# Weight tiles split into a high and a low part by two GpSimd transfers instead of a staged load, a ScalarE cast and a VectorE subtraction

## The chip, the cores and the metric

The kernel runs on one core of one Trainium2 chip. Its engines are PE (TensorE: matmuls, with PEld for the load of the stationary operand), DVE (VectorE), ACT (ScalarE), POOL (GpSimd) and SP (SyncE, which only issues transfers). Transfers between HBM and the on-chip memory run on 16 DMA engines, from queues of SP, ACT and POOL. Each engine works through its own instructions in order and waits on semaphores for the others. The metric is the device time of one launch in microseconds; lower is better.

## What is computed

A decoder trunk of two layers on one sequence: 512 tokens, width 1024, all in float32. The first layer mixes tokens by a gated DeltaNet, the second by sliding-window attention on a shared K/V; each layer ends with a gated MLP with a short causal convolution.

```python
for layer in range(DEPTH):
    if layer < N_A_LAYERS:
        h = h + gated_deltanet(rmsnorm(h, a_norm_w[i]), a_w_in[i], ..., a_w_out[i])
    else:
        if j == 0:
            k_sh, v_sh = shared_kv(h, kv_norm_w, w_kv)
        h = h + sliding_window_sink_attention(rmsnorm(h, b_norm_w[j]), k_sh, v_sh, b_w_q[j], ..., b_w_o[j], ...)
    h = h + conv_gated_mlp(rmsnorm(h, ffn_norm_w[layer]), ffn_w_up[layer], ..., ffn_w_down[layer])
return rmsnorm(h, final_norm_w)
```

The weight matrices concern us here: `a_w_in` (1024 x 6176), `a_w_out` (2048 x 1024), `w_kv` (1024 x 512), `b_w_q` and `b_w_o` (1024 x 1024 each), and for each layer `ffn_w_up` (1024 x 5632) and `ffn_w_down` (2816 x 1024). Each weight is used once, against all 512 tokens.

## The kernel before

**Precision by three matmuls.** TensorE takes its operands in a rounded form of float32, here type F32R. To keep more of the precision, each operand is split in two: the high part is the value rounded, the low part is the value minus the high part. A product is then three matmuls, high x high, high x low and low x high (`mm3`, lines 132 to 137), all added into one bank of PSUM. Activations are split by `split` and `split_scaled`, weights by `cast`.

**The path of a weight before.** `load_stage` (L116) has SP load a part of a matrix, kt x 128 rows by 256 columns, into a buffer "stage" (two buffers). `cast` (L124) is called twice for each stage, for its left and its right 128 columns: ScalarE writes the rounded high part into a "whi" tile (L128), VectorE the rest into a "wlo" tile (L129), with three buffers each. `mm3` uses a pair of them for kt x 3 matmuls of 128x128 by 128x512. One such pair and its matmuls is called a block below. kt is 8 nearly everywhere; the down projections of the MLPs are cut into pieces of 6 and 5.

**The stages.** The first, to about 480 us, is the DeltaNet mixer: 48 blocks of `a_w_in` (`project`, L234) among many small matmuls, transposes and a triangular solve, in an order that the list `ORDER` gives. Then come the output projection (L776, 16 blocks), the first MLP (`ffn`, L829: 44 up blocks and 32 down blocks), the attention (L954: 4 blocks for K/V, 8 for the queries in between the attention's own work, 8 for the output), the second MLP and the final norm. In the MLP each up block is followed by `up` (L838): VectorE empties the bank (L842), ScalarE and VectorE do the convolution (L845, L847), and ScalarE the activation (L862) or the product's split (L864, L140).

**What sets the order.** A scheduler places the instructions of each engine from the program's order and from priorities, under the number of buffers that each tag has. A tile whose tag has n buffers can be written again once the tile n places before it was used for the last time. Each engine, and so each queue from which an engine issues transfers, then runs in the order that was fixed. POOL before has 47 small instructions, fills and masks, among them fills of the DeltaNet's tiles (L495, L496, L572) and of the attention's key tiles (L960, L961).

The gates' small weights (`gst`, L250) take the same path with 48 columns and their own load.

Of the kernel before, what the change touches and what calls it, by code (L numbers as in the profile page):

```python
# [8 lines left out]
F32 = mybir.dt.float32  # L9
F32R = mybir.dt.float32r  # L10
BF16 = mybir.dt.bfloat16
AF = mybir.ActivationFunctionType
ALU = mybir.AluOpType
# [4 lines left out]
P = 128  # L18
# [6 lines left out]
HQK = 8  # L25
# [16 lines left out]
def kernel(  # L42
# [27 lines left out]
    V, S, G, PE, SP = nc.vector, nc.scalar, nc.gpsimd, nc.tensor, nc.sync  # L70
# [6 lines left out]
    def nm(s):  # L77
        cnt[0] += 1
        return f"{s}_{cnt[0]}"

    wpool = ctx.enter_context(tc.tile_pool(name="weights", bufs=1, side="right"))
# [32 lines left out]


    def load_stage(w, r0, kt, c0):  # L116
        st = wpool.tile([P, 8, 256], F32, tag="stage", bufs=2, name=nm("stage"))
        SP.dma_start(
            st[:, :kt, :],
            w[r0 : r0 + kt * P, c0 : c0 + 256].rearrange("(k p) c -> p k c", p=P),  # L120
        )
        return st

    def cast(st, kt, half, m=P):  # L124
        hi = wpool.tile([P, 8, P], F32R, tag="whi", bufs=3, name=nm("whi"))
        lo = wpool.tile([P, 8, P], F32R, tag="wlo", bufs=3, name=nm("wlo"))
        src = st[:, :kt, half * P : half * P + m]
        S.copy(hi[:, :kt, :m], src)  # L128
        V.tensor_tensor(lo[:, :kt, :m], src, hi[:, :kt, :m].bitcast(F32), op=ALU.subtract)  # L129
        return hi, lo  # L130
# [20 lines left out]
        SP.dma_start(xt[:], x[0, c * P : (c + 1) * P, :])  # L151
        xs.append(xt)
    win = a_w_in[0]
    first = wpool.tile([P, 8, 256], F32, tag="stage", bufs=2, name=nm("stage"))
    for i in range(2):
        cs = slice(HQK * P + i * P, HQK * P + (i + 1) * P)
        SP.dma_start(first[:, :, i * P : (i + 1) * P], win[:, cs].rearrange("(k p) c -> p k c", p=P))
    held_stage = {HQK * P: first}


    ident = const([P, P], s="ident")
# [71 lines left out]
    st = [{} for _ in range(4)]  # L233
    def project(c0, i):  # L234
        if c0 not in held_stage:
            held_stage[c0] = load_stage(win, 0, 8, c0)
        ps = bank("d")
        mm3(ps[:], cast(held_stage[c0], 8, i), KD, xh, xl)
        return ps
# [7 lines left out]


    QKV = 2 * HQK * P + HV * P
    gst = wpool.tile([P, 8, 256], F32, tag="stage", bufs=2, name=nm("gst"))  # L250
    G.memset(gst[:, :, 0:48], 0.0)
    c_b = QKV + HV * P
    S.dma_start(gst[:, :, 0:16], win[:, c_b : c_b + 16].rearrange("(k p) c -> p k c", p=P))
    S.dma_start(gst[:, :, 32:48], win[:, c_b + 16 : c_b + 32].rearrange("(k p) c -> p k c", p=P))
    gw = cast(gst, KD, 0, m=48)
    gps = bank("d")
    mm3(gps[:48, :], gw, KD, xh, xl, m=48)
# [19 lines left out]
    for c in range(NC):  # L277
        cs = slice(c * P, (c + 1) * P)
        V.tensor_tensor_scan(R[32:48, cs], ones[32:48, 0:P], sp_r[32:48, cs], 0.0, op0=ALU.mult, op1=ALU.add)
    for c in range(NC):  # L280
        cs = slice(c * P, (c + 1) * P)
# [494 lines left out]
    for m2 in range(KD // 2):  # L776
        sts = [load_stage(a_w_out[0], 1024 * u, 8, 256 * m2) for u in range(2)]
        for j in range(2):
            m = 2 * m2 + j
            ps = bank("d")  # L780
            for u in range(2):
                w = cast(sts[u], 8, j)
                mm3(ps[:], w, 8, yh[8 * u : 8 * u + 8], yl[8 * u : 8 * u + 8], first=u == 0, last=u == 1)
            V.tensor_tensor(hT[m], hT[m], ps[:], op=ALU.add)
# [44 lines left out]
    def ffn(l, h, last=False):  # L829
# [22 lines left out]
        for t0, t1 in ((0, 12), (12, 22)):  # L852
            gh, gl = [], []
            for t in range(t0, t1, 2):
                if l == 0 and t == 6:
                    bias_rows()
                sg = load_stage(wup, 0, 8, t * P)
                sv = load_stage(wup, 0, 8, DFF + t * P)
                gp, lp = wide("G"), wide("L")
                for j in range(2):  # L860
                    a = up(cast(sg, 8, j), t + j, "ga")
                    S.activation(a[:], a[:], AF.Silu)  # L862
                    b = up(cast(sv, 8, j), NF + t + j, "va")
                    V.tensor_tensor(b[:], a[:], b[:], op=ALU.mult)  # L864
                    split(b[:], gp[:, j, :], lp[:, j, :])
                    gh.append(gp[:, j, :])
                    gl.append(lp[:, j, :])
            ku = (t1 - t0) // 2
            for m2 in range(KD // 2):
                sts = [load_stage(wdn, (t0 + u * ku) * P, ku, 256 * m2) for u in range(2)]  # L870
                for j in range(2):
                    m = 2 * m2 + j
                    ws = [cast(sts[u], ku, j) for u in range(2)]
                    if last and t1 == NF and m == KD - 1:
                        final(h, lambda ps, ts, u: down(ps, ws, ku, gh, gl, ts, u))
                        continue
                    ps = bank("d")
                    for u in range(2):
                        down(ps[:], ws, ku, gh, gl, slice(0, T), u)
                    V.tensor_tensor(h[m], h[m], ps[:], op=ALU.add)  # L880
# [247 lines left out]
```

## Time and profile before

| | |
|---|---|
| time, median of 3 runs | 1462.74 us (1460.52 to 1462.97) |
| the profiled execution | 1458.21 us, span 1456.4 us from the first to the last instruction |
| mean granted TensorE clock | 0.996 |
| instructions | 19,545 |
| HBM read, written | 134.65 MB, 16.80 MB |
| SP's queue of transfers | 160,722 packets, 151.27 MB, 33.3% of the 16 DMA engines' span |

Busy time is the time in which an engine had an instruction in work. Matmuls are pipelined: a single matmul of 128x512 shows some 400 ns while the next one starts earlier, so the rate is read from the distance of starts or of finished blocks, not from the mean of one. "Idle before, releaser" is the time for which an engine stood before an instruction, and what ended the wait. An instruction's line with "q" behind the engine (SPq) is one of the queue that issues. "To landing" is the time from the issue of a transfer to the point at which its data can be used. In the table of windows each row gives a stretch of time, and how long each engine was busy in it.

### The profile page before, as it was taken

To read this page: it belongs to the slowest core of one execution; us is meant where nothing else is said; L and a number is where in the kernel's file an instruction comes from. 1 tells how busy PE (TensorE), PEld (TensorE's weight loads), DVE (VectorE), ACT (ScalarE), POOL (GpSimd) and SP (SyncE) were. 2 spreads that over 40 slices of the span, in tenths; PEclk is the share of its full clock that TensorE was granted. 3 is DMA by queue.
4 is the path that set the end of the run, shared out by engine and by line. 5 is a ranking of instruction groups with operands and counts; after the bars stand their busy time and mean duration, and the time that the engine had idled before them with its cause. 6 is when DMAs were issued, how large, how long until landed. Compare 5 with 4: busy or idle time off the path is not lost.

```text
span 1456.4 us, 19545 instructions
## 1 busy us (share of the span) xinstructions
PE 1432.3 (98%) x7519; PEld 1163.6 (80%) x7519; DVE 953.5 (65%) x1661; ACT 718.9 (49%) x1406; POOL 20.1 (1%) x47
## 2 busy tenths in 40 slices
PE   7999999999999999999999999999999999999998
PEld 5778877888877788888888888877788888888887
DVE  5896885978844436776247765777757774366754
ACT  7764564656646424443224444578744443234433
POOL 1000000000000000000010000000000000000000
PEclk9999999999999999999999999999999999999999
DMA  5334254163366523232232234221132322322222
GB/s 154 92 99 112 78 171 119 59 189 110 98 189 209 163 87 108 69 114 87 87 116 91 83 95 130 89 79 44 58 105 69 116 83 86 122 87 87 94 73 94
DMA packets 163074, 152.71 MB, mean 105 GB/s; under 512 B 24165, under 2 KB 150694, under 8 KB 162982
## 3 DMA queue, kind: packets, MB, share of 16 engines
q1 hardware_dynamic: 160722, 151.27, 33.3%
q8 instruction: 59, 0.97, 0.3%
q10 hardware_dynamic: 2259, 0.20, 0.2%
q14 instruction: 34, 0.27, 0.1%
HBM read 134.65 MB, written 16.80 MB: 104 GB/s over the span
## 4 chain that ended last, share of the span: by engine, by line
PE 95%; DMA 3%; ACT 1%; DVE 1%; issue 0%; ACTq 0%; DVEq 0%; SPq 0%
PE d L135 27%; PE d L137 27%; PE d L136 26%; PE s L585 2%; PE p L1043 1%; PE s L600 1%; PE g L1038 1%; PE s L625 1%; PE p L608 1%; PE s L562 1%; PE p L555 1%; PE s L1013 1%; PE g L450 1%; PE g L671 1%; PE g L375 1%; DMA ol<-od 0%
## 5 line engine op out<-in xcount | busy, mean ns | idle before, releaser
L135 PE MATMUL d<-xh,whi 128*128 128x512 f32 x1192 | 475.8, 400 | 0.1
L137 PE MATMUL d<-xh,wlo 128*128 128x512 f32 x1192 | 473.3, 398 | 0.0
L136 PE MATMUL d<-xl,whi 128*128 128x512 f32 x1192 | 471.6, 396 | 0.0
L128 ACT CAST whi<-stage 128x1024 fp32r<-128x1024 f32 (+2 forms) x236 | 230.5, 979 | 337.6 <-PE d L136 318.6
L129 DVE TENSOR_TENSOR wlo<-stage,whi 128x1024 fp32r<-128x1024 f32 (+2 forms) x236 | 267.3, 1133 | 120.4 <-ACT whi L128 114.3
L137 PEld LDWEIGHTS d<-xh,wlo 128*128 128x128 f32 x1192 | 224.4, 188 | 50.5 <-issue 1.4
L136 PEld LDWEIGHTS d<-xl,whi 128*128 128x128 f32 x1192 | 224.3, 188 | 48.2 <-issue 1.2
L135 PEld LDWEIGHTS d<-xh,whi 128*128 128x128 f32 x1192 | 224.7, 188 | 46.1 <-issue 0.7
L842 DVE TENSOR_TENSOR sz<-d,p6s 128x512 f32<-128x512 f32 x58 | 40.0, 689 | 62.9 <-PE d L137 61.0
L227 DVE SCALAR_TENSOR_TENSOR acc<-d,cwc,acc 128x511 f32<-128x511 f32 (+2 forms) x96 | 70.7, 740 | 9.3 <-ACT acc L224 8.8
L862 ACT ACTIVATE dt<-dt 128x512 f32<-128x512 f32 x44 | 27.8, 632 | 83.5 <-DVE dt L847 83.5
L135 PE MATMUL d<-sy,whi 128*128 128x512 f32 (+1 forms) x148 | 57.6, 390 | 0.0
L137 PE MATMUL d<-sy,wlo 128*128 128x512 f32 (+1 forms) x148 | 57.5, 389 | 0.0
L135 PE MATMUL d<-kT,whi 128*128 128x512 f32 (+1 forms) x146 | 57.5, 396 | 0.0
L136 PE MATMUL d<-sy,whi 128*128 128x512 f32 (+1 forms) x148 | 57.0, 385 | 0.0
L137 PE MATMUL d<-kT,wlo 128*128 128x512 f32 (+1 forms) x146 | 57.0, 390 | 0.0
L136 PE MATMUL d<-qT,whi 128*128 128x512 f32 (+1 forms) x146 | 56.8, 389 | 0.0
L847 DVE SCALAR_TENSOR_TENSOR va<-sz,fcw,va 128x511 f32<-128x511 f32 (+1 forms) x58 | 43.4, 748 | 2.7 <-ACT va L845 1.7
L847 DVE SCALAR_TENSOR_TENSOR dt<-sz,fcw,dt 128x511 f32<-128x511 f32 (+1 forms) x58 | 43.4, 748 | 1.2 <-ACT dt L845 0.2
L842 DVE TENSOR_TENSOR zl<-d,p6s 128x512 f32<-128x512 f32 x30 | 20.7, 689 | 33.4 <-PE d L137 33.1
L507 DVE TENSOR_TENSOR sT<-sT,p6s 64x31 f32<-64x31 f32 (+15 forms) x124 | 40.9, 330 | 2.0
L501 DVE TENSOR_TENSOR p6s<-sN,sT 64x31 f32<-64x31 f32 (+15 forms) x124 | 40.9, 330 | 1.8
(377 smaller groups left out, 2116.8 us busy)
## 6 DMA issues: line engine op xcount, KB each, us to landing
stage<-in_ffn_w_up_dram SPq DMA_DIRECT2D x44, 1024.0 KB, 5.1
stage<-in_a_w_in_dram SPq DMA_DIRECT2D x23, 1024.0 KB, 5.4
stage<-in_ffn_w_down_dram SPq DMA_DIRECT2D x16, 768.0 KB, 4.3
stage<-in_ffn_w_down_dram SPq DMA_DIRECT2D x16, 640.0 KB, 4.1
stage<-in_a_w_out_dram SPq DMA_DIRECT2D x8, 1024.0 KB, 5.0
zd<-sz SPq DMA_DIRECT2D x16, 256.0 KB, 2.1
od<-o SPq DMA_DIRECT2D x16, 256.0 KB, 2.5
stage<-in_b_w_q_dram SPq DMA_DIRECT2D x4, 1024.0 KB, 5.0
```

The costliest lines, as they stand in the source:

```text
L128: S.copy(hi[:, :kt, :m], src)
L129: V.tensor_tensor(lo[:, :kt, :m], src, hi[:, :kt, :m].bitcast(F32), op=ALU.subtract)
L135: PE.matmul(ps, hi[:, k, :m], xh[k], start=first and k == 0, stop=False)
L136: PE.matmul(ps, hi[:, k, :m], xl[k][:], start=False, stop=False)
L137: PE.matmul(ps, lo[:, k, :m], xh[k], start=False, stop=last and k == kt - 1)
L227: V.scalar_tensor_tensor(acc[:, d:], ps[:, : T - d], col, acc[:, d:], op0=ALU.mult, op1=ALU.add)
L501: V.tensor_tensor(tv, N[:, s, s + 1 : 32].unsqueeze(2).to_broadcast([64, n, m]), Tm[:, s : s + 1, 0:m].to_broadcast([64, n, m]), op=ALU.mult,)
L507: V.tensor_tensor(Tm[:, s + 1 : 32, 0:m], Tm[:, s + 1 : 32, 0:m], tv, op=ALU.subtract)
L585: PE.matmul(x[:, si], t[:, i, cs], S0[:, si], start=True, stop=True)
L842: V.tensor_tensor(u[:], ps[:], rs[:], op=ALU.mult)
L847: V.scalar_tensor_tensor(acc[:, d:], u[:, : T - d], tap(2 - d, t), acc[:, d:], op0=ALU.mult, op1=ALU.add)
L862: S.activation(a[:], a[:], AF.Silu)
```

## The change

`load_stage` no longer loads: it hands on the address of the weights in HBM. For the 236 blocks of 128 columns, `cast` now issues a transfer from POOL's queue that reads the weights from HBM and writes them rounded into the high tile (the type differs on the two sides); ScalarE writes the negative of the high tile into the low tile; and a second transfer from POOL's queue reads the same weights from HBM again and adds them to the low tile. VectorE has no part in it. The high and the low tiles have four buffers each instead of three, and the two stage buffers are gone but for one that holds the gates' weights, which keep the old path. The two half loads with which SP began are gone too.

```diff
     def load_stage(w, r0, kt, c0):
-        st = wpool.tile([P, 8, 256], F32, tag="stage", bufs=2, name=nm("stage"))
-        SP.dma_start(
-            st[:, :kt, :],
-            w[r0 : r0 + kt * P, c0 : c0 + 256].rearrange("(k p) c -> p k c", p=P),
-        )
-        return st
+        return w[r0 : r0 + kt * P, c0 : c0 + 256].rearrange("(k p) c -> p k c", p=P)
 
     def cast(st, kt, half, m=P):
-        hi = wpool.tile([P, 8, P], F32R, tag="whi", bufs=3, name=nm("whi"))
-        lo = wpool.tile([P, 8, P], F32R, tag="wlo", bufs=3, name=nm("wlo"))
+        hi = wpool.tile([P, 8, P], F32R, tag="whi", bufs=4, name=nm("whi"))
+        lo = wpool.tile([P, 8, P], F32R, tag="wlo", bufs=4, name=nm("wlo"))
         src = st[:, :kt, half * P : half * P + m]
+        if m == P:
+            G.dma_start(hi[:, :kt, :], src)
+            S.activation(lo[:, :kt, :], hi[:, :kt, :].bitcast(F32), AF.Copy, scale=-1.0)
+            G.dma_start(lo[:, :kt, :], src, accum_op=ALU.add)
+            return hi, lo
         S.copy(hi[:, :kt, :m], src)
         V.tensor_tensor(lo[:, :kt, :m], src, hi[:, :kt, :m].bitcast(F32), op=ALU.subtract)
         return hi, lo
...
-    first = wpool.tile([P, 8, 256], F32, tag="stage", bufs=2, name=nm("stage"))
-    for i in range(2):
-        cs = slice(HQK * P + i * P, HQK * P + (i + 1) * P)
-        SP.dma_start(first[:, :, i * P : (i + 1) * P], win[:, cs].rearrange("(k p) c -> p k c", p=P))
-    held_stage = {HQK * P: first}
+    held_stage = {}
...
-    gst = wpool.tile([P, 8, 256], F32, tag="stage", bufs=2, name=nm("gst"))
+    gst = wpool.tile([P, 8, 256], F32, tag="stage", bufs=1, name=nm("gst"))
```

The transfers now stand in POOL's order. The next rows are POOL's in the up projection of the second MLP; a name's number counts the tiles, so that a wlo belongs to the whi one number below it. Line 124 is the transfer of the high part, line 126 the accumulating one. Before, POOL's last work was the fills for the attention, and nothing followed them up to the end of the program:

```order
L960 MEMSET ktok_7608 64x512
L961 MEMSET ktok_7608 64x512
L960 MEMSET ktok_7609 64x512
L961 MEMSET ktok_7609 64x512
L1124 UNCONDITIONAL_BRANCH
L1124 ISA
```

```order
L124 DMA whi_10746<-in_ffn_w_up_dram 128x8x128
L126 DMA wlo_10710<-in_ffn_w_up_dram 128x8x128
L124 DMA whi_10785<-in_ffn_w_up_dram 128x8x128
L126 DMA wlo_10747<-in_ffn_w_up_dram 128x8x128
L124 DMA whi_10822<-in_ffn_w_up_dram 128x8x128
L126 DMA wlo_10786<-in_ffn_w_up_dram 128x8x128
L126 DMA wlo_10823<-in_ffn_w_up_dram 128x8x128
```

Here the high part of a later block is issued ahead of the accumulation of the block before it. In the output projection of the DeltaNet mixer POOL's order is another; each accumulation stands directly behind its own block's high part, and the fills of the solve's tiles (L568) are in between:

```order
L124 DMA whi_4627<-in_a_w_out_dram 128x8x128
L126 DMA wlo_4628<-in_a_w_out_dram 128x8x128
L124 DMA whi_4656<-in_a_w_out_dram 128x8x128
L126 DMA wlo_4657<-in_a_w_out_dram 128x8x128
L124 DMA whi_4687<-in_a_w_out_dram 128x8x128
L126 DMA wlo_4688<-in_a_w_out_dram 128x8x128
L568 MEMSET Xg 32x8x32
L124 DMA whi_4716<-in_a_w_out_dram 128x8x128
L568 MEMSET Xg 32x8x32
L126 DMA wlo_4717<-in_a_w_out_dram 128x8x128
```

POOL had no transfer at this place. The third place is ScalarE in an MLP's up projection; before, the cast of a block (L128) stands between the activations of earlier blocks:

```order
L845 ACTIVATE va_9473<-sz_9471,normc_101,fcw_377 128x512
L128 CAST whi_9560<-stage_9554 128x1024
L140 CAST kT_9404<-va_9473 128x512
L128 CAST whi_9596<-stage_9556 128x1024
L845 ACTIVATE dt_9511<-sz_9509,normc_101,fcw_377 128x512
```

After, the negative (L125) stands in the cast's place (L841 is the old L845), three to four blocks ahead of the matmuls that use its tile:

```order
L841 ACTIVATE va_10854<-zl_10852,normc_98,fcw_375 128x512
L140 CAST nt_10707<-va_10854 128x512
L125 ACTIVATE wlo_10977<-whi_10976 128x1024
L841 ACTIVATE dt_10895<-sz_10893,normc_98,fcw_375 128x512
L858 ACTIVATE dt_10895<-dt_10895 128x512
L125 ACTIVATE wlo_11018<-whi_11017 128x1024
L841 ACTIVATE va_10932<-sz_10930,normc_98,fcw_375 128x512
```

What moved is what ScalarE waits for there: before, for a stage that was loaded and a high tile that was free; now for the high tile's transfer and a low tile that is free, and POOL's accumulation waits for it in turn.

## The prediction

> **What bounds the kernel now.** I read the busy shares first, then the chain that ended last, then the stages, and only then the engines that the change touches.
>
> ```profile
> PE 1432.3 (98%) x7519; PEld 1163.6 (80%) x7519; DVE 953.5 (65%) x1661; ACT 718.9 (49%) x1406; POOL 20.1 (1%) x47
> PE 95%; DMA 3%; ACT 1%; DVE 1%; issue 0%; ACTq 0%; DVEq 0%; SPq 0%
> 0.00:480.00 480.00, 462.90 (x3031) 377.71 (x3032) 348.70 (x732) 290.63 (x707) 11.74 (x31) 0.99 0.44 130
> 480.00:550.00 70.00, 69.57 (x313) 56.51 (x312) 32.57 (x39) 26.92 (x36) 0.00 (x0) 1.00 0.34 109
> 550.00:920.00 370.00, 370.00 (x1621) 302.45 (x1621) 227.22 (x292) 146.14 (x186) 8.34 (x16) 1.00 0.31 99
> 937.00:1040.00 103.00, 103.00 (x625) 76.74 (x625) 80.83 (x253) 78.47 (x243) 0.00 (x0) 1.00 0.18 55
> PE g L182 <- DMA acc<-in_ffn_conv_b_dram: 9.2, 1, 9.2
> ```
>
> The window rows give the stretch, its length, the busy time of PE, weight load, DVE, ACT and POOL, the granted clock, the DMA share and GB/s. TensorE is busy in all of the first MLP (550 to 920) and of the attention core (937 to 1040); the clock is full. The whole idle time of PE is 1456.4 - 1432.3 = 24.1 us, 17.1 of it in the DeltaNet stage (0 to 480), and of that 9.2 us are the first wait, for a load. So freed ACT and DVE time can bring little; the question is whether weights still arrive in time. POOL, nearly idle, gets the work.
>
> How often does PE want a weight tile? A "block" is one hi/lo pair, kt tiles of 128x128 deep, three matmuls for each tile.
>
> ```profile
> 604.28 0.69 DVE L842 TENSOR_TENSOR sz<-d,p6s 128x512 f32<-128x512 f32 x1 [1.96 <-PE d L137]
> 605.01 0.82 ACT L845 ACTIVATE va<-sz,normc,fcw 128x512 f32<-128x512 f32 x1
> 608.57 0.62 ACT L140 CAST sy<-va 128x512 fp32r<-128x512 f32 x1 [2.74 <-DVE va L864]
> 615.27 0.69 DVE L842 TENSOR_TENSOR sz<-d,p6s 128x512 f32<-128x512 f32 x1 [1.46 <-PE d L137]
> ```
>
> L842 empties a finished block. From 604.28 to 615.27 two blocks pass: 5.50 us for kt = 8, or **0.687 us a tile**; so 4.12 us for kt = 6 and 3.43 for kt = 5.
>
> **What goes.** SP's weight loads, ScalarE's cast (kept in another form) and VectorE's subtraction:
>
> ```profile
> L129 DVE TENSOR_TENSOR wlo<-stage,whi 128x1024 fp32r<-128x1024 f32 x172 | 210.3, 1224 | 64.0 <-ACT whi L128 58.2 <-PE d L135 1.6 <-PE d L137 0.3
> L128 ACT CAST whi<-stage 128x1024 fp32r<-128x1024 f32 x172 | 180.4, 1052 | 193.0 <-PE d L136 178.4 <-DMA stage<-in_a_w_in_dram 4.2 <-issue 4.0
> L128 ACT CAST whi<-stage 128x768 fp32r<-128x768 f32 x32 | 26.8, 836 | 84.2 <-PE d L136 84.2
> L128 ACT CAST whi<-stage 128x640 fp32r<-128x640 f32 x32 | 23.3, 729 | 60.4 <-PE d L136 56.0 <-PE d L137 3.0 <-DMA stage<-in_ffn_w_down_dram 1.4
> SPq L118 <- DVE wlo L129: 852.0, 99, 29.6
> ```
>
> There are 172 blocks of kt = 8, 32 of 6 and 32 of 5: 236 blocks, 1,728 tiles. All of it lies beside PE: ACT waited for PE's release (178.4 of 193.0 us before the large casts), and SP waited 852 us for a stage buffer, so loads ran ahead of need. Removing 267 us from DVE is worth 0 while PE is full. ScalarE's negative has the cast's shape and is priced at its 1.05 us, hidden by the same slack.
>
> **What comes.** Each block has two transfers on POOL's queue, each of kt x 128 pieces of 512 bytes: 2,048 pieces for a kt = 8 block, where before a 1 MB load with 1 KB pieces served two blocks. Three costs follow.
>
> *The DMA engines.* The first load of before already has 512-byte rows; between 8.3 and 10.3 us it runs almost alone.
>
> ```profile
> DMA packets 1165, 0.59 MB, mean 294 GB/s; under 512 B 16, under 2 KB 1165, under 8 KB 1165
> stage<-in_ffn_w_up_dram SPq DMA_DIRECT2D x44, 1024.0 KB, 5.1
> stage<-in_ffn_w_down_dram SPq DMA_DIRECT2D x16, 640.0 KB, 4.1
> 600.90 0.37 SPq L118 DMA_DIRECT2D stage<-in_ffn_w_up_dram  x1
> ```
>
> 1,165 packets in 2.0 us is 1.72 ns each, 0.22 us for the 128 of a tile. The first transfer costs that. No row shows an accumulating one: from 0.22 (a copy) to 0.66 us a tile (the destination read and written besides). I take 0.44, nearer the copy, since only one more read is certain; together 0.66 of 0.687 us. That is barely hidden.
>
> *The time from issue to landing.* 1,024 KB land in 5.1 us and 640 KB in 4.1, so 384 KB take 1.0 us; 640 KB then take 1.67, and 4.1 - 0.37 issue - 1.67 leaves about 2.1 us after the last piece. In the MLP a lo buffer comes free with block k-4, and ACT's in-order queue reaches the negative behind that block's last activation, 609.19 - 604.28 = 4.9 us later. Then 1.05 us of negative leaves 3 x 5.50 - 5.95 = 10.5 us for the accumulation: enough up to about 8 us of issuing. Four buffers hide the latency; they do not add throughput.
>
> *The issuing.* SP hands over 1,024 pieces in 0.37 us, 0.36 ns each. No row shows a transfer that POOL issues; the nearest rows are POOL's own writes and its smallest operation:
>
> ```profile
> 2.54 1.80 POOL L336 MEMSET Xg<- 128x2048 f32 x1
> L293 POOL MEMSET sk<- 128x16 f32 x1 | 0.1, 107 | 0.0
> L961 POOL MEMSET kT<- 64x512 f32 x1 | 0.5, 522 | 0.0
> ```
>
> A memset writes a word per partition in 1.80 us / 2048 = 0.88 ns. My estimate: POOL writes four words a piece (from where, to where, how much, control; an assumption), 3.5 ns, plus 0.1 us a transfer (L293). Ends: SP's 0.36 ns, and 7.0 ns if the read and the write side are written one after the other. I take 3.5, as nothing yet says the sides go by turns: 1,024 x 3.52 + 100 = **3.7 us a transfer**, 7.4 us a kt = 8 block; 5.6 for kt = 6 and 4.7 for kt = 5. All exceed PE's 5.50, 4.12 and 3.43. POOL becomes the bound wherever blocks follow one another.
>
> Its queue is also in order. In the MLPs the order puts another block's first transfer ahead of most accumulations, so landing and negative are covered. In the output projection and most of the DeltaNet stage the order is hi, lo, hi, lo: the lo stands waiting for landing and negative, with the next hi behind it, and a block lasts 3.7 + 2.1 + 1.05 + 3.7 = 10.55 us.
>
> **The sum**, against the profiled execution (span 1456.4, run 1458.2, so 1.8 around it):
> - Each MLP has 44 blocks of kt = 8 and 16 each of 6 and 5: 44 x 7.4 + 16 x 5.6 + 16 x 4.7 = 490 against 363 on PE: +127, twice: +255.
> - Key/value and attention output, 12 blocks: 12 x (7.4 - 5.5) = +23. The 8 query blocks lie beside 103 us of attention, 59 us of issuing: 0.
> - Output projection, 16 blocks: half in the serial order, 8 x 5.05, half 8 x 1.9: +55.
> - DeltaNet stage, 48 blocks in 480 us: serial 506 us: +26. This cover is thin: PE's own other work hides it.
> - Start: the first hi transfer competes with x, but carries half of the old 1 MB: 0, from -2 to +4.
>
> Together +359: span 1815, run 1817. The profiled run lies 4.5 us below the median 1462.74, so I predict **1820 us**.
>
> **The rivals.**
> 1. *The cover holds.* If POOL writes a piece below 2.6 ns in pairs (5.50 / 2 = 2.75 less 0.1, over 1,024) and below 1.05 ns in serial places, PE stays the bound: about 1463. For it: SP's 0.36 ns and the memset's 0.88. DMA: Bandwidth & Descriptors in the Trainium skill ("Anatomy of one DMA") says that many descriptors can be emitted before the incremental cost shows; by that rule the time is this rival's, and no POOL transfer is in the trace to test it. Chance 0.12.
> 2. *Faster.* The same, and the freed DVE and ACT close gaps outside the start's wait: of 24.1 us at most 15, likelier 5, so about 1458. It needs transfers that issue as SP's do. Chance 0.04.
> 3. *The DMA engines set the pace*, if the accumulation takes three passes: 0.88 us a tile against 0.687: +0.193 x 1,056 tiles = 204 in the MLPs, 18 for the 96 tiles of the attention's dense blocks and 25 for the projection's 128, with POOL fast enough: about 1710. Chance 0.12.
> 4. *DVE holds POOL up.* Two selects of one shape differ:
>
> ```profile
> 1.44 0.29 POOL masks.py:199 TENSOR_SCALAR_AFFINE_SELECT ident<-ident 128x128 f32<-128x128 f32 x1
> 18.25 0.61 POOL L300 TENSOR_SCALAR_AFFINE_SELECT acc<-acc 128x128 f32<-128x128 f32 x1
> 18.16 0.55 DVE L129 TENSOR_TENSOR wlo<-gst,whi 128x384 fp32r<-128x384 f32 x1
> 550.00:920.00 370.00, 82.60 (x77) 1.00 0.31 99
> ```
>
> The second runs beside a VectorE subtraction and takes twice as long. The last row is L129's part of DVE's time in the first MLP. If POOL stands in all that remains, (227.22 - 82.60) / 370 = 39%, a transfer takes 3.7 / 0.61 = 6.1 us, a block 12.2; and by the steps of the sum the MLPs gain 2 x 444, the DeltaNet stage 257, the projection 133 and the attention 80: +1358, so 2820. The Trainium skill's SBUF — State Buffer ("Who interferes with whom") agrees with these rows: a VectorE instruction with two SBUF inputs blocks a GpSimd instruction that reads SBUF, and it warns of descriptors held up. Chance 0.08.
> 5. *Both sides by turns*, 7.0 ns: 7.3 us a transfer; MLPs +1206, DeltaNet +373, projection +171, attention +123: about 3335. For it, that each piece needs both sides; against it, only that nothing shows them in turn. Chance 0.10.
>
> **How the numbers follow.** My forecast, POOL's issuing as the bound with 2.6 to 6 ns a piece, has 0.54. Its own range is 1500 to 2600. The range reaches from 1465, over rivals 3 and 4, to 3000; it leaves out rival 5 (0.10), rival 2 and the part of rival 1 below it (0.10). A difference of 0.2% is about what a measurement of this kernel can tell. Faster: 0.04; same: half of rival 1, 0.06; slower: 0.90.
>
> **What would show it.** POOL's queue should hold 472 weight transfers back to back in the MLPs, PE's busy share should fall to about 79%, and PE should wait at L135 for whi and at L137 for wlo, with the POOL transfer as releaser. The two transfers of an MLP block should come 7.4 us apart per block. If POOL's queue is idle between transfers while the DMA share is near 1, rival 3 is right; if transfers grow with DVE work beside them, rival 4. The forecast is wrong if PE keeps 98%.

## The result, and the profile after

The changed kernel takes **1878.85 us** (median of 4 runs, 1874.80 to 1885.29) against 1461.63 for the kernel before (median of 4, 1455.45 to 1462.97): a ratio of 1.287, with an interval of 1.282 to 1.292. The forecast was 1820 with a range of 1465 to 3000, so the time lies inside it, 3% above the forecast. The reason given for it was wrong all the same.

The first lines are from the page of the changed kernel: the span, the busy shares, the chain that ended last, three groups (busy time and mean ns of one, then the idle time of the engine ahead of them and who ended it), and the transfers of the high parts (the last number is the median from issue to landing).

```profile
span 1876.9 us, 19997 instructions
PE 1574.3 (84%) x7519; PEld 1237.2 (66%) x7519; DVE 712.3 (38%) x1425; ACT 710.9 (38%) x1405; POOL 593.6 (32%) x519
issue 27%; POOL 13%; DMA 11%; PE 7%; ACT 2%; DVE 1%; POOLq 0%; ACTq 0%; DVEq 0%
L126 POOL DMA_DIRECT2D wlo<-in_ffn_w_up_dram x88 | 138.6, 1575 | 415.2 <-ACT wlo L125 414.5
L125 ACT ACTIVATE wlo<-whi 128x1024 fp32r<-128x1024 f32 (+2 forms) x236 | 232.1, 984 | 824.2 <-DMA whi<-in_ffn_w_up_dram 269.7
L137 PE MATMUL d<-xh,wlo 128*128 128x512 f32 x1192 | 504.3, 424 | 102.3 <-DMA wlo<-in_ffn_w_up_dram 95.2
...
whi<-in_ffn_w_up_dram POOLq DMA_DIRECT2D x88, 512.0 KB, 8.1
```

PE is no longer the bound: its share fell from 98% to 84% and its part of the chain from 95% to 7%. POOL, which the forecast made the bound, is busy for only 32% of the span. Its accumulations took 138.6 us in the up projections and stood 415.2 us ahead of that, for ScalarE's negative. The negative itself stood for the high part's transfer. PE waited at L137 for the low part: it is the last in a row of three.

The list of waits says the same for the whole program (total us, times, longest):

```profile
POOL wlo L126 <- ACT wlo L125: 940.3, 190, 11.1
ACT wlo L125 <- DMA whi<-in_ffn_w_up_dram: 269.7, 52, 10.5
ACT wlo L125 <- DMA whi<-in_a_w_in_dram: 148.2, 32, 11.2
PE g L437 <- ACT va L438: 19.5, 4, 11.4
PE g L476 <- ACT va L224: 19.0, 8, 5.1
```

POOL stood 940.3 us, half of the span, for 190 of its 236 negatives. The last two rows are from the DeltaNet stage: there PE waited for ordinary work of ScalarE. In the longest of these waits, 11.4 us up to 321.24, that work (L438) stood in ScalarE's queue behind a negative that had waited 8.7 us for its high part.

One period shows the mechanism. These are POOL's instructions, then ScalarE's, in the first MLP's up projection; in brackets the wait ahead of the instruction and its releaser.

```profile
769.35 2.48 POOL L124 DMA_DIRECT2D whi<-in_ffn_w_up_dram  x2
779.36 1.56 POOL L126 DMA_DIRECT2D wlo<-in_ffn_w_up_dram  x1 [7.53 <-ACT wlo L125]
783.37 1.57 POOL L126 DMA_DIRECT2D wlo<-in_ffn_w_up_dram  x1 [2.45 <-ACT wlo L125]
784.26 2.48 POOL L124 DMA_DIRECT2D whi<-in_ffn_w_up_dram  x2
```

```profile
777.98 1.06 ACT L125 ACTIVATE wlo<-whi 128x1024 fp32r<-128x1024 f32 x1 [6.17 <-DMA whi<-in_ffn_w_up_dram]
778.95 0.80 ACT L841 ACTIVATE dt<-sz,normc,fcw 128x512 f32<-128x512 f32 x1
781.41 0.63 ACT L858 ACTIVATE dt<-dt 128x512 f32<-128x512 f32 x1 [1.67 <-DVE dt L843]
781.95 1.04 ACT L125 ACTIVATE wlo<-whi 128x1024 fp32r<-128x1024 f32 x1
```

At 769.35 two high parts are issued, one behind the other. The first lets ScalarE go at 777.98, 8.6 us later. Its negative is done at 779.04, and POOL issues the accumulation at 779.36. The second negative must stay behind L841 and L858 in ScalarE's queue, and L858 waits for a VectorE step; so it ends at 782.99, and its accumulation goes at 783.37. Only then do the next two high parts leave, at 784.26, since they stand behind that accumulation on POOL. One round trip, issue, landing, negative, issue, serves two blocks and cannot start before the last one has ended. Two of them last from 769.35 to 798.20, or 14.4 us each: **7.2 us a block against PE's 5.50**. The stretch is typical: where two accumulations of up blocks follow one another, their starts lie 7.3 us apart on the mean of both MLPs. The DMA engines meanwhile run dry, as the rate from 760 to 800 us shows, one number for each microsecond:

```profile
GB/s 261 326 289 172 16 0 5 133 183 180 34 135 182 185 281 318 300 145 17 0 0 27 157 176 156 36 161 177 193 272 309 299 138 19 2 15 154 183 179 50
```

In each trip three or four microseconds have less than 30 GB/s.

The windows (stretch, length, busy time of PE, weight load, DVE, ACT, POOL, then granted clock, DMA share, GB/s) add a second cost:

```profile
0.00:626.50 626.50, 515.93 (x3070) 412.75 (x3071) 298.95 (x680) 295.12 (x713) 148.08 (x142) 0.90 0.84 147
698.00:1208.00 510.00, 417.60 (x1638) 324.97 (x1638) 148.87 (x216) 145.29 (x190) 198.55 (x174) 0.92 1.03 142
780.00:786.00 6.00, 2.30 (x10) 1.58 (x10) 4.08 (x6) 2.28 (x3) 3.55 (x4) 1.00 0.74 92
786.00:793.00 7.00, 7.00 (x25) 5.15 (x24) 1.29 (x2) 1.64 (x3) 0.74 (x1) 0.76 1.53 221
788.00:789.00 1.00, 1.00 (x3) 0.73 (x3) 0.00 (x0) 0.00 (x0) 0.00 (x0) 0.50 1.46 193
```

In the third row PE stood for 3.7 of 6 us; in the fourth it is busy throughout, at a mean clock of 0.76, and one microsecond of it, the fifth row, has 0.50. So this gap is paid for twice. In the DeltaNet stage (first row) and the first MLP (second) PE stands 111 and 92 us at a mean clock of 0.90 and 0.92. Over the program PE's idle time grew from 24.1 to 302.6 us (1876.9 - 1574.3), and its busy time, for the same 7,519 matmuls, from 1432.3 to 1574.3: 278 us of standing and 142 us more of busy time make up the 420 us of the two spans. The clock accounts for that busy time: a mean of 0.917 over 1876.9 us loses 156 us against full speed, 0.996 over 1456.4 us loses 6, and a part of the difference falls into gaps. TensorE: Matmul & The Clock Gate in the Trainium skill (Part 1) says that about 3.4 us without work halve the clock until a busy window of that length has passed. The last two rows agree: by that rule we estimate a mean of 1 - 0.5 x 3.4 / 7 = 0.76 over the 7 us, and the clock of the fifth row is half.

Where the time went, by stage. A stage ends with its first or last emptied bank; the rows of these two stages, before and then after, are

```profile
L784 DVE TENSOR_TENSOR h<-h,d x4: 680/690/690, 486.3 to 503.3; 128x512 f32<-128x512 f32 x4
L784 DVE TENSOR_TENSOR pz<-pz,d x4: 690/690/690, 514.3 to 547.3; 128x512 f32<-128x512 f32 x4
L780 DVE TENSOR_TENSOR h<-h,d x4: 680/688/690, 626.5 to 646.5; 128x512 f32<-128x512 f32 x4
L780 DVE TENSOR_TENSOR pz<-pz,d x4: 689/690/690, 657.5 to 698.2; 128x512 f32<-128x512 f32 x4
```

so the DeltaNet stage lasts to 626.5 and the output projection to 698.2; before, to 486.3 and 547.3. The attention's first and last emptied banks end the other stages.

| us | before | after | more | forecast |
|---|---|---|---|---|
| DeltaNet stage | 486.3 | 626.5 | +140 | +26 |
| output projection | 61.0 | 71.7 | +11 | +55 |
| first MLP | 374.0 | 510.2 | +136 | +127 |
| attention | 159.1 | 179.4 | +20 | +23 |
| second MLP, final norm | 376.0 | 489.1 | +113 | +127 |

In the DeltaNet stage most of the loss is there when the last weights of `a_w_in` leave. The first row is SP's loads before, the second POOL's accumulations after; the rest is POOL's queue behind them.

```profile
L118 SPq DMA_DIRECT2D stage<-in_a_w_in_dram x23: 368/384/794, 18.8 to 386.6; - x23
L126 POOL DMA_DIRECT2D wlo<-in_a_w_in_dram x48: 1536/1550/2296, 12.7 to 505.2; - x48
506.08 1.58 POOL L124 DMA_DIRECT2D whi<-in_a_w_out_dram  x1
517.41 1.54 POOL L126 DMA_DIRECT2D wlo<-in_a_w_out_dram  x1 [9.75 <-ACT wlo L125]
518.30 1.56 POOL L124 DMA_DIRECT2D whi<-in_a_w_out_dram  x1
```

The 48 accumulations start 10.5 us apart on the mean, and the last one leaves 119 us later than the last load did before. In the serial order of the last three rows one block takes 12.2 us, and eight of the projection's sixteen high parts leave before 626.5, within the DeltaNet stage.

### The profile page after: what moved, and what is told of

The parts are those of the page before. It is cut to its first block, busy times and chain, and to the rows that moved or that the text cites. A ratio compares the mean times of both kernels' runs of the same rounds, so it can differ in the third digit from the quotient of the medians.

```text
span 1876.9 us, 19997 instructions
## 1 busy us (share of the span) xinstructions
PE 1574.3 (84%) x7519; PEld 1237.2 (66%) x7519; DVE 712.3 (38%) x1425; ACT 710.9 (38%) x1405; POOL 593.6 (32%) x519
## 4 chain that ended last, share of the span: by engine, by line
issue 27%; POOL 13%; DMA 11%; PE 7%; ACT 2%; DVE 1%; POOLq 0%; ACTq 0%; DVEq 0%
POOL whi L124 7%; POOL wlo L126 6%; DMA whi<-in_ffn_w_up_dram 5%; DMA whi<-in_ffn_w_down_dram 3%; PE d L137 2%; PE d L136 2%; PE d L135 2%; ACT wlo L125 2%; DMA whi<-in_b_w_q_dram 1%; DMA wlo<-in_ffn_w_down_dram 1%; DMA whi<-in_b_w_o_dram 0%; DVE dt L843 0%; DMA wlo<-in_b_w_o_dram 0%; DMA wlo<-in_ffn_w_up_dram 0%; DMA wlo<-in_w_kv_dram 0%
## 5 line engine op out<-in xcount | busy, mean ns | idle before, releaser
L137 PE MATMUL d<-xh,wlo 128*128 128x512 f32 x1192 | 504.3, 424 | 102.3 <-DMA wlo<-in_ffn_w_up_dram 95.2
L125 ACT ACTIVATE wlo<-whi 128x1024 fp32r<-128x1024 f32 (+2 forms) x236 | 232.1, 984 | 824.2 <-DMA whi<-in_ffn_w_up_dram 269.7
L135 PE MATMUL d<-xh,whi 128*128 128x512 f32 x1192 | 498.1, 419 | 1.1 <-ACT xh L144 1.1
L136 PE MATMUL d<-xl,whi 128*128 128x512 f32 x1192 | 498.7, 419 | 0.3 <-DVE xl L145 0.3
L137 PEld LDWEIGHTS d<-xh,wlo 128*128 128x128 f32 x1192 | 239.7, 201 | 174.2 <-DMA wlo<-in_ffn_w_up_dram 113.6
L135 PEld LDWEIGHTS d<-xh,whi 128*128 128x128 f32 x1192 | 240.1, 202 | 55.2 <-issue 2.5
L126 POOL DMA_DIRECT2D wlo<-in_ffn_w_up_dram x88 | 138.6, 1575 | 415.2 <-ACT wlo L125 414.5
L126 POOL DMA_DIRECT2D wlo<-in_a_w_in_dram x48 | 75.7, 1614 | 236.7 <-ACT wlo L125 203.4
L126 POOL DMA_DIRECT2D wlo<-in_ffn_w_down_dram x64 | 95.3, 1522 | 173.8 <-ACT wlo L125 173.3
L124 POOL DMA_DIRECT2D whi<-in_ffn_w_up_dram x88 | 116.9, 1553 | 12.0 <-PE d L137 12.0
L124 POOL DMA_DIRECT2D whi<-in_a_w_in_dram x48 | 54.6, 1151 | 120.5 <-PE d L137 59.4
L137 PE MATMUL d<-kT,wlo 128*128 128x512 f32 (+1 forms) x146 | 63.2, 433 | 28.8 <-DMA wlo<-in_ffn_w_down_dram 25.9
L124 POOL DMA_DIRECT2D whi<-in_ffn_w_down_dram x64 | 79.7, 1349 | 13.9 <-PE d L137 12.7
L135 PE MATMUL d<-sy,whi 128*128 128x512 f32 (+1 forms) x148 | 60.5, 410 | 10.0 <-ACT sy L140 10.0
L135 PE MATMUL d<-kT,whi 128*128 128x512 f32 (+1 forms) x146 | 60.6, 416 | 7.8 <-ACT kT L140 7.8
L137 PE MATMUL d<-sy,wlo 128*128 128x512 f32 (+1 forms) x148 | 60.4, 408 | 6.6 <-DMA wlo<-in_a_w_out_dram 6.6
```

Source lines behind the costliest of these rows:

```text
L124: G.dma_start(hi[:, :kt, :], src)
L125: S.activation(lo[:, :kt, :], hi[:, :kt, :].bitcast(F32), AF.Copy, scale=-1.0)
L126: G.dma_start(lo[:, :kt, :], src, accum_op=ALU.add)
L135: PE.matmul(ps, hi[:, k, :m], xh[k], start=first and k == 0, stop=False)
L136: PE.matmul(ps, hi[:, k, :m], xl[k][:], start=False, stop=False)
L137: PE.matmul(ps, lo[:, k, :m], xh[k], start=False, stop=last and k == kt - 1)
```

## The experiments

Three theories were set against one another. **A**: the DMA engines set the pace, since an accumulation is slow. **B**: the round trip on POOL's in-order queue sets it. **C**, the forecast's: POOL's issuing sets it, 3.7 us a transfer. The kernel before was run beside each group: 1459.65, 1456.80 and 1456.73 us (medians of 7). Diffs are against the changed kernel unless said otherwise.

### The disputed costs alone

A kernel that does nothing but transfers of 512 KB, eight of one kind in a row: no trunk is computed.

```diff
+    for n in range(N):
+        G.dma_start(view(pr[n], 128), src(n, 128))
+    pause()
+    for n in range(N):
+        G.dma_start(view(pr[n], 128), src(n, 128), accum_op=ALU.add)
...
```

> Computes nothing of the trunk: eight transfers of 512 KB of weights at a time, in groups that follow one another: SP copy in 512-byte pieces; POOL copy; POOL rounding copy; POOL accumulation (rounded and float32 destination); POOL rounding copy and accumulation in 1 KB pieces; accumulation in 4 KB pieces; rounding copies and accumulations by turns. Three theories on the change: A (the DMA engines' rate: an accumulation occupies them far longer than a copy), B (the round trip: POOL's in-order queue stands until the high part has landed and ScalarE has written its negative, with the next high part behind it), C (POOL's issuing). SP's copies should take 1.76 us each by all. A: an accumulation takes 5 to 6 us each back to back, about three times a copy. B: at most 3.5 us each (two reads instead of one). C: a copy from POOL takes 3.7 us each against SP's 1.76.

The first three rows are POOL's eight rounding copies, its eight accumulations, and eight more in 128 pieces of 4 KB (shortest, median and longest duration in ns, first and last start); the other two are windows inside the copies that SP issued and inside POOL's accumulations (POOL busy, clock, DMA share, GB/s).

```profile
L99 POOL DMA_DIRECT2D big<-in_a_w_in_dram x8: 887/914/951, 36.2 to 42.3; - x8
L102 POOL DMA_DIRECT2D big<-in_a_w_in_dram x8: 1574/3938/5974, 54.6 to 61.2; - x8
L114 POOL DMA_DIRECT2D big<-in_a_w_in_dram x8: 877/2032/3207, 153.1 to 156.9; - x8
4.00:14.00 10.00, 0.00 (x0) 1.00 1.18 296
58.00:78.00 20.00, 9.16 (x6) 1.00 1.44 178
```

Eight copies start over 6.1 us and eight accumulations over 6.6, so one follows another after **0.87 and 0.94 us**: issuing 1,024 pieces of 512 bytes costs POOL about 0.9 us, a quarter of the 3.7 of theory C. Accumulations in 128 pieces start 0.54 us apart, so most of the cost goes with the transfer and some 0.4 ns with each piece. (The long durations of the accumulations overlap; starts are the measure.) 512 KB at 178 GB/s are 2.95 us against 1.77 at 296: an accumulation costs the DMA engines 1.66 times a copy, not three times as A needs. A kt = 8 block then needs 1.8 us of POOL and some 4.7 us of the DMA engines, both below PE's 5.50. C falls, A falls in its strong form.

### A plain second copy in place of the accumulation

```diff
-            G.dma_start(lo[:, :kt, :], src, accum_op=ALU.add)
+            G.dma_start(lo[:, :kt, :], src)
```

The subtraction is left out: the low tile receives the weights themselves. All waits stay.

> The second transfer is a plain rounding copy instead of an accumulation, with every wait kept; the low part is then the weights themselves, so the subtraction is left out. A: the engines' time per block falls by half or more and with it the time, to 1600 us or less. B: the round trip stays, only the landings are shorter: 1700 us or more. C: unchanged, 1880.

1651.2 us, ratio 1.132 (1.127 to 1.137): between the two, so it decides nothing alone. POOL still stood for the negative:

```profile
POOL wlo L126 <- ACT wlo L125: 818.0, 204, 10.3
whi<-in_ffn_w_up_dram POOLq DMA_DIRECT2D x88, 512.0 KB, 6.4
```

818 of the 940 us of waiting remain, so the trip still sets the pace; but a high part, which shared the DMA engines with accumulations, now lands in 6.4 us instead of 8.1. The slow accumulation thus lengthens the trip. B had priced that too low, and A gets a share, as a part of the round trip.

### The round trip cut

ScalarE fills the low tile from a tile of zeros, so the negative no longer waits for the high part; both transfers, the accumulation and the order of a block stay. The subtraction is left out. The gates' tile is made smaller to hold the zeros.

```diff
-            S.activation(lo[:, :kt, :], hi[:, :kt, :].bitcast(F32), AF.Copy, scale=-1.0)
+            S.activation(lo[:, :kt, :], zero[:, :kt, :], AF.Copy, scale=-1.0)
```

> ScalarE writes the low tile from a tile of zeros instead of from the high tile, so the accumulation waits no more for the high part's landing; the accumulation stays. The subtraction of the high part is left out; the gates' weights have a smaller tile. A: unchanged, 1800 to 1880 us, DMA share near 1. B: down to 1600 us or less. C: unchanged.

1514.74 us in the profiled execution. (A second execution took 4820.68 us, which is not explained, so what follows rests on a single execution.) The stages after the DeltaNet mixer are back at the times before: 59.1, 373.8, 159.5 and 376.2 us. The same transfers, the same bytes and the same issuing, without the dependence, leave PE the bound in the MLPs, though each of the MLPs' 152 accumulations now stands directly behind its own high part. What is left, 58 us, is in the DeltaNet stage (544.4 against 486.3).

### Six high tiles

The sharpest test of B with the right arithmetic: the chain stays, but the high parts may be issued further ahead. To make room the gates' weights use a row of another tag.

```diff
-        hi = wpool.tile([P, 8, P], F32R, tag="whi", bufs=4, name=nm("whi"))
+        hi = wpool.tile([P, 8, P], F32R, tag="whi", bufs=6, name=nm("whi"))
...
-    gst = wpool.tile([P, 8, 256], F32, tag="stage", bufs=1, name=nm("gst"))
+    gst = row("ol")[:, 0:384].rearrange("p (k m) -> p k m", k=8)
```

> Six buffers for the high parts instead of four (room for them from the gates' weights, which move to a tile of the main pool); everything else is the change. In POOL's queue the high part is now issued three blocks before the accumulation that it stands next to, so it has landed and been negated when the accumulation's turn comes. B (round trip): both MLPs fall from 510 and 489 us to about 380 each, the attention to 160; the DeltaNet stage stays above before's; in all 1520 to 1590. A (the engines' rate; 1.79 us a copy and 2.95 us an accumulation of 512 KB as measured, 4.7 of PE's 5.5 us a block, made worse by sharing): the MLPs stay at 440 us or more each, in all above 1680.

**1516.42 us, ratio 1.042 (1.038 to 1.045).** Two more tiles take back 362 of the 417 us. POOL's queue and the windows of this kernel:

```profile
702.04 0.89 POOL L124 DMA_DIRECT2D whi<-in_ffn_w_up_dram  x1 [2.59 <-PE d L137]
703.46 1.56 POOL L126 DMA_DIRECT2D wlo<-in_ffn_w_up_dram  x1 [0.53 <-ACT wlo L125]
707.53 0.89 POOL L124 DMA_DIRECT2D whi<-in_ffn_w_up_dram  x1 [2.52 <-PE d L137]
```

```profile
0.00:546.00 546.00, 488.25 (x3065) 393.76 (x3065) 297.61 (x681) 295.89 (x714) 149.18 (x144) 0.96 0.99 170
606.00:981.00 375.00, 374.32 (x1639) 305.70 (x1638) 152.70 (x217) 147.75 (x190) 194.33 (x172) 1.00 1.28 190
```

A high part now leaves every 5.49 us, released by PE, which is the bound again: 374.3 of 375 us of the first MLP, at full clock. The wait of the accumulations for the negative is 0.5 us in these rows, since that block's high part landed long ago: at 150 of the MLPs' 152 accumulations two other blocks' high parts are out besides its own, where the changed kernel has one (79 times) or none (73 times). As with the round trip cut, all that is left is in the DeltaNet stage: 545.9 us, +59.6.

### Three tiles of each

```diff
-        hi = wpool.tile([P, 8, P], F32R, tag="whi", bufs=4, name=nm("whi"))
-        lo = wpool.tile([P, 8, P], F32R, tag="wlo", bufs=4, name=nm("wlo"))
+        hi = wpool.tile([P, 8, P], F32R, tag="whi", bufs=3, name=nm("whi"))
+        lo = wpool.tile([P, 8, P], F32R, tag="wlo", bufs=3, name=nm("wlo"))
```

> Three buffers for each part, as before the change, instead of four; the pairs of transfers in POOL's order stay. If the buffers' release is in the loop that sets the pace, the MLPs grow by a fifth or more: 2050 us or above. If POOL's order alone sets it (one round trip for two blocks): 1880 to 1950.

2019.54 us, ratio 1.387 (1.379 to 1.394), between the two expectations. The release of the tiles by PE joins the loop: POOL's high parts wait 471.8 us for PE's release at L137, where the changed kernel has 162.0. The order in the MLPs is that of the changed kernel, 79 and 73 times. So this run says that tiles matter, and not more.

### The negative on VectorE

```diff
-            S.activation(lo[:, :kt, :], hi[:, :kt, :].bitcast(F32), AF.Copy, scale=-1.0)
+            V.tensor_scalar(lo[:, :kt, :], hi[:, :kt, :].bitcast(F32), -1.0, None, op0=ALU.mult)
```

> VectorE writes the negative instead of ScalarE. ScalarE's queue drops out of the round trip, but the scheduler now puts nearly every accumulation directly behind its own block's high part. If ScalarE's in-order queue is the larger part of the round trip: 1700 to 1800 us. If the stand of POOL's queue for the high part's landing is (B): about 1850 to 2050, each serial MLP block lasting some 9 to 10 us (1 issue, 5 landing, 1 negative, 1.5 issue, and the wait for a free engine). A: unchanged, 1880.

2026.09 us, ratio 1.391 (1.386 to 1.396), as B forecast. The negative is shorter (0.68 us instead of 0.98, means over all shapes), ScalarE is free of it, and the time is 147 us longer. So ScalarE's queue is not the larger part of the trip. The order changed too: 104 of the MLPs' 152 accumulations instead of 73 have no other block's high part out, as in POOL's rows of the first MLP. VectorE's queue now stands for the landing in ScalarE's place, and no run separates the two effects.

```profile
825.46 1.56 POOL L124 DMA_DIRECT2D whi<-in_ffn_w_up_dram  x1
834.25 1.54 POOL L126 DMA_DIRECT2D wlo<-in_ffn_w_up_dram  x1 [7.23 <-issue]
835.13 1.56 POOL L124 DMA_DIRECT2D whi<-in_ffn_w_up_dram  x1
```

There a round trip serves one block, 835.13 - 825.46 = 9.7 us. ("Issue" as the releaser says only that the profile shows no wait that ended there.)

### One transfer, and the subtraction on VectorE

The high part by POOL's rounding transfer, the weights a second time by a load of SP, and VectorE's subtraction as before the change: no dependence between two transfers. The gates' tile moves as in the run with six high tiles.

```diff
-            S.activation(lo[:, :kt, :], hi[:, :kt, :].bitcast(F32), AF.Copy, scale=-1.0)
-            G.dma_start(lo[:, :kt, :], src, accum_op=ALU.add)
+            raw = wpool.tile([P, 8, P], F32, tag="raw", bufs=2, name=nm("raw"))
+            SP.dma_start(raw[:, :kt, :], src)
+            V.tensor_tensor(lo[:, :kt, :], raw[:, :kt, :], hi[:, :kt, :].bitcast(F32), op=ALU.subtract)
...
-    gst = wpool.tile([P, 8, 256], F32, tag="stage", bufs=1, name=nm("gst"))
+    gst = row("ol")[:, 0:384].rearrange("p (k m) -> p k m", k=8)
```

> The high part stays a rounding transfer of POOL; the weights come a second time by SP in 512-byte pieces, and VectorE subtracts as before the change. No accumulation, no round trip, the same bytes. A and B: PE is the bound again, 1455 to 1480 us. C: POOL has half the transfers, about 1470 too by 3.7 us a block; if POOL's issuing were slower than that it would show here alone.

1542.54 us, ratio 1.058 (1.054 to 1.063): a miss. 54 of the 82 us between the spans are again in the DeltaNet stage (540.5), 10 in the projection and 10 in the first MLP. So the DeltaNet stage loses without any accumulation too, which the three theories did not foresee.

### What the DeltaNet stage loses

Its remaining loss, 58 to 60 us where the round trip is out of the way, was taken apart with three kernels. In the first, the stage and the output projection take the old path (SP's load of 128 columns into two tiles, cast, subtraction), the rest that of the run with the round trip cut; the subtraction is left out after the projection.

```diff
+    staged = [True]
...
-        if m == P:
+        if m == P and not staged[0]:
...
+        if m == P:
+            raw = wpool.tile([P, 8, P], F32, tag="raw", bufs=2, name=nm("raw"))
+            SP.dma_start(raw[:, :kt, :], src)
+            src = raw[:, :kt, :]
```

> As e4_no_round_trip (the low tile is written from zeros, so the subtraction is left out), but the DeltaNet stage and its output projection take their weights by the old path (SP load in 512-byte pieces, ScalarE cast, VectorE subtraction). e4 lost 58 us before the MLP and nothing behind it. If those are the weight transfers' in that stage: 1455 to 1475 us. If they come from something else that e4 changed (buffers, the gates' tile, the load order): 1500 or more.

1480.64 us, ratio 1.016 (1.013 to 1.019). The stage takes 518.3 us: 26 less than with the new path's transfers, 32 more than before: between the two expectations. The other two change the kernel **before** in what this run shares with others: the gates' tile in another row (as with six high tiles), and loads of 128 columns. For the latter the first block's own loads are left out, and the gates' tile is one of the four new ones.

```diff
-    gst = wpool.tile([P, 8, 256], F32, tag="stage", bufs=2, name=nm("gst"))
+    gst = row("ol")[:, 0:384].rearrange("p (k m) -> p k m", k=8)
```

> The kernel before, with one thing moved: the gates' weights use a row of tag ol instead of a stage buffer. Nothing is left out. Two theories of the 32 us that the old path in the DeltaNet stage still lost (518.3 against 486.3 us). Theory G (the gates' tile in a row of the stage's own work, and the order of the stage that comes with it): this kernel loses most of it, 1480 to 1495, DeltaNet stage 505 to 520. Theory L (the loads of 128 columns in pieces of 512 bytes): this kernel loses nothing, 1455 to 1468. Since the run without the round trip kept a gates' tile of its own and the one with six high tiles did not, and their DeltaNet stages took 544.4 and 545.9, I expect L.

```diff
-        st = wpool.tile([P, 8, 256], F32, tag="stage", bufs=2, name=nm("stage"))
...
+            raw = wpool.tile([P, 8, P], F32, tag="raw", bufs=4, name=nm("raw"))
+            SP.dma_start(raw[:, :kt, :], src)
+            src = raw[:, :kt, :]
```

> The path of the kernel before everywhere (SP's load, ScalarE's cast, VectorE's subtraction, three high and three low tiles), but each load brings 128 columns in pieces of 512 bytes, into four tiles of half the size, and the first block has no load of its own ahead. Nothing is left out. Theory L (pieces of 512 bytes, loads per block): it loses 15 to 35 us, all in the DeltaNet stage (500 to 520), with the stage's own transfers landing later. Theory G (the gates' tile and the order): it loses nothing, 1455 to 1468. If both this and the other kernel keep 1463, what is left is the number of buffers (two tiles of 128 columns, or four and four high and low tiles) and the order that the scheduler made of it.

1469.46 us (ratio 1.010, 1.008 to 1.013) and 1469.84 us (1.010, 1.006 to 1.015): each loses about 1%, neither G nor L alone. Their DeltaNet stages end at 496.4 and 499.6 us, +10 and +13. The windows over the stage, PE's busy time first: the gates' tile moved, loads of 128, the old path in the stage, and before.

```profile
0.00:496.00 496.00, 473.73 (x3061) 386.31 (x3062) 350.26 (x734) 294.70 (x712) 11.42 (x31) 0.98 0.43 128
```

```profile
0.00:499.00 499.00, 478.87 (x3060) 389.64 (x3061) 349.85 (x734) 293.93 (x711) 11.41 (x31) 0.97 0.46 129
```

```profile
0.00:518.00 518.00, 488.97 (x3080) 395.14 (x3081) 352.00 (x736) 296.70 (x714) 11.42 (x31) 0.96 0.44 124
```

```profile
0.00:486.00 486.00, 468.65 (x3062) 382.07 (x3063) 351.09 (x734) 294.08 (x713) 11.74 (x31) 0.99 0.44 131
```

Against before, PE is busy 5, 10 and 20 us longer for the same work and stands 5, 3 and 12 us more; with six high tiles it is 20 longer and 40 more (the row above: 546 - 488.25 = 57.75 against 17.35). So the new path's transfers in the stage cost some 29 us of standing. There the stage's own small transfers through HBM land later, beside a DMA share of 0.99 instead of 0.44; before (and again with the old path in the stage), then with six high tiles:

```profile
nd<-nt SPq DMA_DIRECT2D x64, 16.0 KB, 1.5
```

```profile
nd<-nt SPq DMA_DIRECT2D x64, 16.0 KB, 2.7
```

That fits, and how many of the 29 us it makes was not tried alone. The slower matmuls at a clock of 0.96 stay with the old path. The two small edits make 23 of the 32 us if they add up, which no run shows; and against a fixed price of the gates' row speaks that the run with the round trip cut has a gates' tile of its own and loses no less than the one with six high tiles. What all these kernels share is that the scheduler places the stage's instructions otherwise. So of the stage's 60 us, some 26 go with the new path's transfers there, by the single execution without the round trip (28 by the kernel with six high tiles); the rest stays open.

## Why the prediction was right, and where it was wrong

**What bounds the kernel now** was right: PE at 98%, nothing to gain from freed DVE and ACT time. VectorE lost 241 us of work, and no stage became faster.

**Issuing: the step that failed.** The prediction took 3.7 us a transfer and made POOL the bound. Measured: 0.9 us, for a copy and for an accumulation alike. The term was mis-sized in its parts: 3.5 ns a piece and 0.1 us a transfer were taken, and some 0.4 ns and 0.5 us came out. The condition of rival 1, below 2.6 ns a piece in pairs (and below 1.05 in serial places), was thus met at 0.9 ns in all. DMA: Bandwidth & Descriptors in the Trainium skill ("Anatomy of one DMA"), which that rival named, says that many descriptors can be emitted before the incremental cost shows. The trace agrees: eight times as many pieces took 0.94 us instead of 0.54. But that rival's time, 1463, did not follow, since the cover failed elsewhere. The transfers were not back to back; POOL stood 940 us.

**Latency: the second step that failed**, and the cause of the time: "in the MLPs the order puts another block's first transfer ahead of most accumulations, so landing and negative are covered". It was so for 79 of 152 accumulations, and even there that other first transfer covers only 0.9 us. The accumulation stands behind it in the same queue until its own high part has landed and been negated, and no further high part can leave meanwhile. The landing was too short besides: 3.7 + 2.1 = 5.8 us from issue to landing by the prediction's terms, 8.1 measured. That fits high parts that stand behind an accumulation on the DMA engines: from 771 us the rate is an accumulation's, 135 to 185 GB/s, and rises to 281 to 318 only after it; with no accumulations a high part landed in 6.4 us. "Four buffers hide the latency" counted the tiles, 10.5 us ahead, and not the queue, in which at most one other block's high part is out. Cutting the dependence, or keeping two other high parts out, brings the MLPs back to 374 to 375 and 376 us; that is shown.

**The negative** was priced at 1.05 us for kt = 8 (1.04 to 1.06 in the rows above) and "hidden by the same slack". Its duration is hidden; its wait is not, as ScalarE's queue stands with it: in the DeltaNet stage PE waited for L438 and L224 of ScalarE, and 148 us of the negatives' wait are there.

**The DMA engines**: a copy at 0.22 us a tile was right (1.77 / 8 = 0.22); the accumulation, taken at 0.44, measured 0.37, so 0.59 of PE's 0.687: hidden, as forecast. Rival 3 was wrong, though the rate counts within the trip: a plain second copy made the kernel 228 us faster.

**The sum.** The MLPs' +255 met +249 by an accident of two sizes: 7.4 us a block from issuing, 7.3 measured from the trip. The attention's +23 met +20. The serial price of 10.55 us a block was also met by luck, from other parts: 10.5 on the mean of the 48 DeltaNet blocks, 12.2 in the projection's serial rows. What failed is what it was set against. The forecast laid 48 blocks, 506 us, over the whole stage of 480 us; but before, the last of their loads leaves at 386.6 us, and 100 us of the stage follow it. With the last accumulation at 505.2, 119 of the stage's +140 us (for +26) were lost by then. The projection's +11 (for +55) is low because half of its transfers leave within the DeltaNet stage. Of the +140, some 80 (626.5 - 545.9) go with the round trip, 26 with the load of the transfers, and the rest is open. "This cover is thin" was right about the place.

**A term that is missing**: PE's clock. 142 of the 420 us are longer busy time for the same matmuls, at a mean clock of 0.917 instead of 0.996.

**Rival 4**, DVE holding POOL up, did not show: with six high tiles a high part took 0.89 us to issue beside a VectorE busy for half of the time (20.8 of the 40 us from 700), against 0.87 to 0.90 in the kernel that has only transfers. **Rival 5** falls with 0.9 us. Among the signs listed, PE's 79% came out as 84%, the waits at L137 came and those at L135 for whi hardly did, and the MLP's up block was 7.3 for 7.4 us.

## What to carry to other kernels

When an engine's in-order queue issues both a transfer and another that depends on its landing, count how many independent transfers stand between the two in that queue, not how many buffers there are: the trip from issue to landing to the second issue sets the pace. Issue the first transfer several blocks ahead, and give it more buffers than the second. In this kernel gaps on PE cost their length and then slower microseconds (278 and 142 us), so gaps in a kernel that PE bounds can be worth more than they look. And when a stage's cover is priced, take the time up to its last load, not the length of the stage.

## What the runs showed of the hardware

- POOL hands over 1,024 pieces of 512 bytes in about 0.9 us, rounding (0.87), accumulating (0.94) or neither (0.90), and 128 pieces of 4 KB in 0.54 us, where SP's issue of a 1 MB load showed 0.37 us.
- An accumulating transfer into the on-chip memory ran at 178 GB/s in 512-byte pieces, SP's plain copy at 296, and a rounding copy takes no longer than a plain one: POOL's ran at 292 and 291.
- After a stretch in which PE stood 3.7 of 6 us, the clock over the next 7 us was 0.76 with PE always busy, and 0.50 in one microsecond of them. Clocks below 1 came without visible gaps too (0.91 from 120 to 200 us with loads of 128 columns, PE busy 79.5 of 80 us), so gaps are not the only cause; which other there is, no run shows.
